# A decoder trunk's third merge: two of its four gate chunks by seven block products, ahead of the pipeline

## The chip, the cores and the metric

The kernel runs on one core of a Trainium2 chip. The metric is the device time of one execution in microseconds (us); the number given for a kernel is the median of its runs. The engines are named as in the profile: PE (TensorE, matrix products into PSUM), DVE (VectorE), ACT (ScalarE), POOL (GpSimd) and SP (SyncE, which issues most of the transfers from device memory).

## What is computed

Two layers of the same kind, on 256 tokens of width 2048 in float32. Each layer normalises its input, multiplies it by one wide input projection, and gives the parts to three token mixers: A (sparse attention), B (a convolution module) and C (stick-breaking attention). Each mixer's output is multiplied by a SiLU gate z and projected back to 2048 columns; the three results are merged by sigmoid gates, and one output projection goes into the residual:

```
y_b = (conformer_conv(ub, ...) * silu(zb)) @ w_b_out
y_c = (stick_breaking_attention(qc, kc, vc) * silu(zc)) @ w_c_out
g = sigmoid(gates).reshape(b, s, N_BRANCH, D_MODEL)
merged = g[:, :, 0] * y_a + g[:, :, 1] * y_b + g[:, :, 2] * y_c
return x + merged @ w_out
```

Here the third summand matters: per layer its gate is a product of the 256 x 2048 activations with 2048 columns of the input projection, and y_c a product of 256 x 1024 with 2048 columns.

## The kernel before

A product of float32 accuracy is made from parts. Every weight block of 256 rows x 512 columns (one **unit**, 128 partitions x 1024 elements) is loaded by SP into a `raw` buffer, rounded by ACT into `wh` (`high`, L251) and its remainder taken by DVE into `wl` (`low`, L255). The activations lie ready in the same two parts, `hx` for the normalised input. A unit's products are activations-high by `wh`, activations-low by `wh`, activations-high by `wl`, for two halves of the tokens (t = 0, 1) and two blocks of 128 rows: 12 matmuls of 128x512 (`token_products`, L265 for every matmul). There are five `raw` buffers, three pairs `wh`, `wl`, and in the pipeline (below) a fourth pair `ph`, `pl`.

The merges of branches A (b = 0) and C (b = 2) are four column chunks j of 512 columns each. Per chunk `chunk_N` makes the gate chunk `g` (8 units, K = 2048), ACT takes the sigmoid, `chunk_N` makes the y chunk (4 units, K = 1024), and DVE multiplies and adds into `mg` (`merge`, L1359 and L1360). The PSUM pool `acc` has two tiles of two banks, the pool `mm` two more. Before j = 3 of branch C stands the gate z of branch B (`gate(O_ZB, ...)`, 16 units): its product is turned over a scratch in device memory (DVE transposes, POOL transfers out and back), then comes a sigmoid on ACT and two multiplications on DVE, all some units later (`LATER`). Its factor `cv` comes from `conv_norm`, a background stage that starts at j = 2. Ahead of j = 3 stand also `hs`, the sums of blocks of `hx`.

Branch B's merge and the output projection run as one list of units (`run`), in which DVE's and SP's order is the order as written; ACT's and PE's order is set by the scheduler of the tile framework. `run` loads a unit 7 places ahead and converts it 3 places ahead. Half of each gate product there (the first 1024 rows of K, two chunks of 512 columns, two halves of tokens) is made by `seven`: seven products of sums of blocks in place of eight, with sums of activation blocks (`hs`) and of weight blocks. One block product is two half units P1a, P1b, P7a, and so on, of 6 matmuls each. Four PSUM banks X, W, Z, Y collect them, X and W in one `mm` tile, Z and Y in the other, and `combine` moves partial results between banks and the buffers V, U1, U2, R5 on DVE (L449); V is copied out by ACT after P1b (L506). Weight blocks are named by block row and column: "11" and "22" are fetched into activation slots (`fetch`, L461), "12" and "21" are loaded as units and also added to "11" by an accumulating transfer of POOL (`grow`, L490), and DVE adds or subtracts "22" (`add`, L464).

Of the kernel before, what the change touches and what calls it, by code (L numbers as in the profile page):

```python
# [14 lines left out]
P = 128  # L15
S = 256
# [32 lines left out]
def trunk(ctx: ExitStack, tc: tile.TileContext, x, w_in, xt, w_a, w_b, w_c, w_out,  # L49
# [39 lines left out]
    def nm(s):  # L89
        uid[0] += 1  # L90
        return f"{s}_{uid[0]}"

    def slot(dt=F32):
        return sp.tile([P, KC, S], dt, tag="s8", bufs=13, name=nm("s8"))

    def long_tile(name):
        return sp.tile([P, LONG], F32, tag="yT", bufs=1, name=nm(name))[:, :KC * (S + PAD)].rearrange("p (k t) -> p k t", k=KC)

    def long_slot():
        return long_tile("long")[:, :, :S]  # L100
# [97 lines left out]
    def finish():  # L198
        while stages:
            advance(stages[0])  # L200
# [129 lines left out]
    def chunk_F(w, c0, act, nk, use, later=LATER):  # L330
        turned(chunk_N(w, [(c0, 512)], act, nk), use, later)
# [40 lines left out]
    def token_products(accs, n, w_, act, k0, ku, nk, ts, banks=False):  # L372
        for i, j in ((0, 0), (1, 0), (0, 1)):
            for t, acc in zip(ts, accs):
                for k in range(ku):
                    a = part(act, i, k0 + k, 1, slice(t * P, (t + 1) * P))[:, 0, :]
                    mm = mult(acc[:, :n], a, w_[j][:, k, :], opens(acc) if banks else k0 + k == 0 and i == 0 and j == 0,
                              k0 + k == nk - 1 and j == 1)
        return mm
# [28 lines left out]

    def plain(w, c0, act, k0, accs, nk, banks=False, ts=range(NT)):
        def products(u):  # L410
            return token_products(accs(), 512, u[1:], act, k0, 2, nk, ts, banks)

        def load():
            u = load_unit(w, k0, 2, [(c0, 512)], weight_parts())
            count[0] -= 1
            return u

        return Unit(load, products)
# [17 lines left out]
    def seven(w, cols, act, sums, banks, keep, by_transfer):  # L436

        X, W, Z, Y = range(4)
        held = {}
        V, U2, U1, R5 = range(4)

        def combine(op, dst, a, b):

            dst, a, b = ({"b": banks, "k": keep}[n][0][i] for n, i in (dst, a, b))
            op(dst, a, b)  # L449

        def block(b, h):
            k, n = (int(i) - 1 for i in b)
            k = k * 4 + h * 2
            return w[k * P:(k + 2) * P, cols[n]:cols[n] + 512].rearrange("(k p) c -> p k c", p=P)

        def fetch(b):
            v = slot().rearrange("p (k a) t -> p k (a t)", a=2)
            with tc.high_priority():
                for h in range(2):
                    held[b, h] = v[:, h * 2:h * 2 + 2, :]  # L460
                    nc.sync.dma_start(held[b, h], block(b, h))  # L461

        def add(h, to, b):
            nc.vector.tensor_add(held[to, h], held[to, h], held[b, h])  # L464

        def sub(h, b, a, k0, t, bank):
            ts = slice(t * P, (t + 1) * P)

            def load():
                if (b, h) not in held:  # L470
                    k, n = (int(i) - 1 for i in b)
                    u = load_unit(w, k * 4 + h * 2, 2, [(cols[n], 512)], weight_parts())
                    count[0] -= 1
                    held[b, h] = u[0]
                    return u
                return (held[b, h], *weight_parts())

            def products(u):
                for i, j in ((0, 0), (1, 0), (0, 1)):
                    for k in range(2):  # L480
                        mm = mult(banks[0][bank], part(a, i, k0 + h * 2 + k, 1, ts)[:, 0, :], u[1 + j][:, k, :],
                                  opens(banks[0][bank]), False)
                return mm

            u = Unit(load, products)
            u.size = 0.5
            return u

        def grow(h, to, b):
            nc.gpsimd.dma_start(held[to, h], block(b, h), accum_op=ALU.add)  # L490

        p1, p2, p4 = (("11", act, 0, 0, X), ("21", act, 4, 0, X), ("11", act, 4, 1, W))
        p5, p6, p3 = (("11", sums, 4, 1, Z), ("11", sums, 0, 0, Y), ("22", sums, 4, 0, Z))
        p7 = ("12", sums, 0, 1, Y)
        order = [p1, p7, p5, p6, p3, p2, p4]
        subs = [sub(h, *v) for v in order for h in range(2)]
        P1, P7, P5, P6, P3, P2, P4 = (subs[n:n + 2] for n in range(0, 14, 2))
        for h in range(2):
            for b, last, at in (("12", P1, P7), ("22", P5, P6), ("21", P6, P4)):
                if b in by_transfer:  # L500
                    last[h].more = [partial(grow, h, "11", b)]
                else:
                    at[h].early = [partial(add, h, "11", b)]
            P7[h].early = [*P7[h].early, partial(add, h, "12", "22")]
        add_, sub_ = nc.vector.tensor_add, nc.vector.tensor_sub
        P1[1].now = [lambda: nc.scalar.copy(keep[0][V], banks[0][X])]  # L506
        P7[1].now = [partial(combine, add_, ("k", U1), ("k", V), ("b", Y))]
        P5[1].now = [partial(combine, sub_, ("k", R5), ("b", Z), ("k", V))]
        P6[1].now = [partial(combine, sub_, ("k", U1), ("b", Y), ("k", U1)),
                     partial(combine, sub_, ("k", U2), ("k", V), ("b", Y))]  # L510
        extra = {(0, 1): U2, (1, 0): U1, (1, 1): R5}
        return fetch, subs, lambda q, t: keep[0][extra[q, t]] if (q, t) in extra else None
# [115 lines left out]
    def gate(c0, o, b, w, hx, done=None, more=2):  # L628
        def use(k, y):
            sg = sigmoid_of(y)  # L630
            yield 1
            while done is not None and done.count(k // 4) < NT:
                advance(stages[0])
            nc.vector.tensor_mul(y, y, sg)
            nc.vector.tensor_mul(y, y, blocks(o[:, k:k + 4, :]).rearrange("p k u i -> p u k i"))
            split(blocks(hi(b, k, 4)), blocks(lo(b, k, 4)), by_feature(y))

        for k in range(0, KC, 4):
            chunk_F(w, c0 + k * P, hx, KD, partial(use, k), LATER + more if k else LATER - 1)

    def tap(yT, cv, pr, c, q):
        wq = pr[:, P_CW + c * TAPS + q:P_CW + c * TAPS + q + 1]
# [46 lines left out]
    for layer in range(DEPTH):  # L689
# [672 lines left out]
        for b in (0, 2):  # L1362
            gx = ga if b == 0 else gc
            for j in range(4):
                if b == 0 and j == 3:
                    gc = parts(KC)
                    gate(O_ZC, qcT, gc, w, hx, stuck)
                if b == 2 and j == 2:
                    flush()
                    start(conv_norm())  # L1370
                if b == 2 and j == 3:
                    finish()
                    gb = parts(KC)
                    gate(O_ZB, cv, gb, w, hx, more=-1)
                    hs, v = parts(KC), long_slot()
                    for i in (0, 4):
                        nc.vector.tensor_add(v[:, i:i + 4, :], hi(hx, i, 4).bitcast(F32), lo(hx, i, 4).bitcast(F32))
                    list(forms(v))
                    for i in (4, 0):
                        split_at(hs, i, 4, v[:, i:i + 4, :])  # L1380
                g = chunk_N(w, [(O_G + b * D + j * 512, 512)], hx, KD)
                sg = [ev() for _ in range(NT)]
                with tc.high_priority():
                    for t in range(NT):
                        nc.scalar.activation(sg[t], g[t], AF.Sigmoid)
                if j == 0:
                    settle()
                y = chunk_N((w_a, w_c)[b // 2][layer], [(j * 512, 512)], gx, KC)
                with tc.high_priority():
                    for t in range(NT):  # L1390
                        merge(b, j, t, y, sg)

        def banks():
            return Lazy(1, lambda: halves([mm_tile(), mm_tile()]))

        og = O_G + D
        units, woven, fetches = [], [], []
        for j in (0, 2):
# [74 lines left out]
        def accs(q):  # L1473
            if q not in acc:
                if q - p0 in (0, 1):
                    acc[q] = o_banks[0][(p0 + 1 - q) * 2:(p0 + 1 - q) * 2 + 2]
                else:
                    acc[q] = token_accs()
            return acc[q]
# [42 lines left out]
                units[n].before = [*units[n].before, partial(fetch, b)]  # L1522
        woven = sorted([*enumerate(units), *woven], key=lambda e: e[0])
        with tc.manual_schedule(engines={nc.vector.engine, nc.sync.engine}):
            run([u for _, u in woven], [])
        if not last:
            continue
        known, half = small(2), small(2)
# [109 lines left out]
```

## Time and profile before

| what | value |
|---|---|
| median of 3 runs | 2005.98 us (2005.85 to 2006.45) |
| the profiled execution's own time | 2004.83 us |
| its span in the profile | 2003.1 us |
| PE busy, matmuls | 1993.5 us (100%), 9314 |
| DVE busy, ACT busy, POOL busy | 82%, 55%, 10% |
| mean DMA rate | 232 GB/s |

The share of busy time is an average over stages. Matmuls are pipelined: one is shown with 0.39 us, but the next begins long before it ends, so the distance from start to start tells what one costs. Times of the trace are counted from the span's start. The place of the change is, in layer 0, the stretch from about 690 to 850 us, and in layer 1 the same about 1000 us later.

### The profile page before, as it was taken

The numbers are of one execution on the slowest core, as the hardware profiler recorded it, in microseconds if no ns is written. First come the engines' busy times: TensorE is split into PE (matmuls) and PEld (weight loads), VectorE is DVE, ScalarE is ACT, GpSimd is POOL, SyncE is SP. The second block draws the span as 40 slices with busy tenths as digits, with TensorE's granted clock in tenths as the row PEclk, the third lists the DMA queues.
The fourth block names the chain that finished last, engine by engine and source line by source line (L and its number), as shares of the span: only waits on it lengthen the run. The fifth ranks groups of instructions, "written<-read, shape, count | busy, mean of one in ns | idle before, by whom it ended". The sixth has DMA issues, their size and how long they took to land.

```text
span 2003.1 us, 25866 instructions
## 1 busy us (share of the span) xinstructions
PE 1993.5 (100%) x9314; PEld 1674.2 (84%) x9314; DVE 1646.5 (82%) x2179; ACT 1107.4 (55%) x1275; POOL 200.5 (10%) x308
## 2 busy tenths in 40 slices
PE   9999999999999999999999999999999999999998
PEld 8889888888888888888888988888888888888886
DVE  8667899878888877798785779988888788778997
ACT  7555555566644455565554555555656445555654
POOL 0111012100010001022110111121000100011120
PEclk9999999999999999999999999999999999999999
DMA  7788578755575567789977885787555765687894
GB/s 279 229 286 266 185 223 291 247 179 186 174 222 192 189 219 253 244 256 281 299 254 231 278 256 184 231 284 247 179 178 173 227 193 190 216 272 241 266 300 160
DMA packets 235585, 463.80 MB, mean 232 GB/s; under 512 B 17280, under 2 KB 30080, under 8 KB 235328
## 3 DMA queue, kind: packets, MB, share of 16 engines
q1 hardware_dynamic: 208768, 389.25, 59.7%
q0 software_dynamic: 25024, 69.75, 12.4%
q10 hardware_dynamic: 1664, 3.15, 0.4%
q8 instruction: 73, 1.20, 0.2%
q14 instruction: 56, 0.46, 0.1%
HBM read 429.31 MB, written 32.77 MB: 231 GB/s over the span
## 4 chain that ended last, share of the span: by engine, by line
PE 98%; DMA 1%; DVE 1%; issue 0%; POOL 0%; ACT 0%; DVEq 0%; POOLq 0%
PE acc L265 80%; PE mm L265 15%; DMA z<-zt 1%; PE mm L1078 1%; PE mm L1168 0%; DMA zy<-z 0%; PE mm L1136 0%; PE mm L1273 0%; PE mm L1219 0%; PE mm L837 0%; DVE wl L255 0%; PE mm L1249 0%; PE mm L1278 0%; PE mm L1222 0%; PE mm L1139 0%
## 5 line engine op out<-in xcount | busy, mean ns | idle before, releaser
L265 PE MATMUL acc<-wh,s 128*128 128x512 f32 (+1 forms) x4712 | 1165.8, 389 | 0.0
L251 ACT CAST wh<-raw 128x1024 fp32r<-128x1024 f32 (+1 forms) x667 | 697.9, 1048 | 704.2 <-PE acc L265 489.8
L255 DVE TENSOR_TENSOR wl<-raw,wh 128x1024 fp32r<-128x1024 f32 (+1 forms) x668 | 808.6, 1213 | 265.0 <-ACT wh L251 262.2
L265 PEld LDWEIGHTS acc<-wh,s 128*128 128x128 f32 x4712 | 876.9, 188 | 172.9 <-issue 0.2
L265 PE MATMUL acc<-wl,s 128*128 128x512 f32 (+1 forms) x2164 | 575.7, 388 | 0.3 <-DVE wl L255 0.3
L265 PEld LDWEIGHTS acc<-wl,s 128*128 128x128 f32 x2164 | 405.7, 188 | 82.6 <-DVE wl L255 0.7
L297 POOL DMA_DIRECT2D z<-zt x180 | 106.1, 602 | 1297.0 <-DVE zt L294 942.2
L647 DVE SCALAR_TENSOR_TENSOR s<-yT,cst,s 128x256 f32<-128x256 f32 x480 | 211.9, 477 | 0.0
L265 PE MATMUL mm<-wh,s 128*128 128x512 f32 x544 | 139.4, 389 | 0.0
L265 PEld LDWEIGHTS mm<-wh,s 128*128 128x128 f32 x544 | 102.1, 188 | 21.2
L265 PE MATMUL mm<-wl,s 128*128 128x512 f32 x272 | 77.7, 389 | 0.0
L265 PEld LDWEIGHTS mm<-s,wl 128*128 128x128 f32 x512 | 66.9, 191 | 5.0
L265 PE MATMUL mm<-s,wl 128*128 128x192 f32 x512 | 66.0, 271 | 0.0
L251 ACT CAST wh<-s 128x1024 fp32r<-128x1024 f32 x43 | 45.3, 1052 | 27.5 <-PE mm L265 13.3
L265 PEld LDWEIGHTS mm<-wl,s 128*128 128x128 f32 x272 | 51.1, 188 | 10.6
L303 POOL DMA_DIRECT2D zy<-z x50 | 36.1, 722 | 236.3 <-DMA z<-zt 72.7
L255 DVE TENSOR_TENSOR wl<-s,wh 128x1024 fp32r<-128x1024 f32 x43 | 52.4, 1218 | 8.9 <-ACT wh L251 8.6
L294 DVE STREAM_TRANSPOSE zt<-acc 128x512 f32<-128x512 f32 (+1 forms) x68 | 45.3, 679 | 9.4 <-PE acc L265 9.4
L251 ACT CAST ph<-raw 128x1024 fp32r<-128x1024 f32 x31 | 32.7, 1054 | 26.8 <-PE mm L265 14.6
L265 PE MATMUL mm<-ph,s 128*128 128x512 f32 x176 | 45.5, 390 | 0.0
L255 DVE TENSOR_TENSOR pl<-raw,ph 128x1024 fp32r<-128x1024 f32 x31 | 37.8, 1218 | 6.9 <-ACT ph L251 6.9
L265 PEld LDWEIGHTS mm<-ph,s 128*128 128x128 f32 x176 | 33.0, 188 | 7.2 <-issue 0.4
(293 smaller groups left out, 1378.9 us busy)
## 6 DMA issues: line engine op xcount, KB each, us to landing
raw<-in_w_in_dram SPq DMA_DIRECT2D x535, 512.0 KB, 4.3
raw<-in_w_out_dram SPq DMA_DIRECT2D x56, 512.0 KB, 6.6
zy<-z POOLq DMA_DIRECT2D x48, 512.0 KB, 5.1
z<-zt POOLq DMA_DIRECT2D x172, 128.0 KB, 4.3
raw<-in_w_a_dram SPq DMA_DIRECT2D x32, 512.0 KB, 3.6
raw<-in_w_c_dram SPq DMA_DIRECT2D x32, 512.0 KB, 4.3
raw<-in_w_b_dram SPq DMA_DIRECT2D x32, 512.0 KB, 5.7
s<-in_w_in_dram SPq DMA_DIRECT2D x16, 512.0 KB, 5.5
```

The source lines that it names most:

```text
L251: newest_parts[0] = nc.scalar.copy(u[1], u[0])
L255: newest_parts[1] = sub = nc.vector.tensor_sub(u[2], u[0], u[1].bitcast(F32))
L265: newest[0] = nc.tensor.matmul(o, lhsT, rhs, start=start, stop=stop, skip_group_check=True)
L294: nc.vector.transpose(tmp[:, t].rearrange("p b k i -> p k b i"), src.rearrange("p k (b c) -> p k b c", b=4, c=32))
L297: nc.gpsimd.dma_start(z[:, :, :, a, :].rearrange("t b c e -> c (t b) e"), tmp[a * 32:(a + 1) * 32].rearrange("c t b k i -> c (t b) (k i)"))
L303: nc.gpsimd.dma_start(y.rearrange("p (t a) k i -> p t (a k i)", a=4), z.rearrange("t b c a e -> (b c) t (a e)"))
L647: nc.vector.scalar_tensor_tensor(o, yT[:, c, q:q + S], wq, o, op0=ALU.mult, op1=ALU.add)
L1078: nc.tensor.matmul(ps[:, q * S:(q + 1) * S], qi[i][:, hd, :], ki[j][:, 0, :], start=n == 0, stop=n == 2)
```

## The change

In the loop over branch C's chunks, j = 2 becomes the last turn. It starts `conv_norm`, makes the gate z of branch B at once, then `hs`, then the two y chunks 2 and 3 (8 units, which stay in the two `acc` tiles), and leaves the loop. The two gate chunks 2 and 3 go to the front of the list of units: the first 1024 rows of K by a call of `seven` (14 half units P1a to P4b), the rest by 8 plain units, X8 to X14 for chunk 3 (banks X, W) and Z8 to Z14 for chunk 2 (banks Z, Y), in an order written by hand. Block "11" is fetched into the buffer `yT` that held the convolution's input, "22" into a slot. Sigmoids and merges follow as `gates_c` and `close_c`. The second half of gate z is used two units earlier than before.

```diff
+    def long_as_slot():
+        return sp.tile([P, LONG], F32, tag="yT", bufs=1, name=nm("block"))[:, :KC * S].rearrange("p (k t) -> p k t", k=KC)
...
         def products(u):
+            if ts == (1, 0):
+                return [token_products(accs()[t:t + 1], 512, u[1:], act, k0, 2, nk, [t], banks) for t in ts][-1]
...
-            chunk_F(w, c0 + k * P, hx, KD, partial(use, k), LATER + more if k else LATER - 1)
+            chunk_F(w, c0 + k * P, hx, KD, partial(use, k), LATER + more if k and more > 0 else LATER - 3 if k else LATER - 1)
...
                 if b == 2 and j == 2:
                     flush()
                     start(conv_norm())
-                if b == 2 and j == 3:
-                    finish()
                     gb = parts(KC)
                     gate(O_ZB, cv, gb, w, hx, more=-1)
+                    finish()
...
+                    y_c = {c: chunk_N(w_c[layer], [(c * 512, 512)], gc, KC) for c in (2, 3)}
+                    break
...
+        g_banks, kept = banks(), Lazy(1, lambda: halves([t4(), t4()]))
+        og = O_G + 2 * D
+        fetch, subs, share = seven(w, (og + 3 * 512, og + 2 * 512), hx, hs, g_banks, kept, ("12", "21"))
+        ahead = {f"P{i}{h}": subs[n * 2 + m] for n, i in enumerate((1, 7, 5, 6, 3, 2, 4)) for m, h in enumerate("ab")}
...
+        def gates_c(q, g_banks=g_banks, kept=kept, share=share):
+            for t in range(NT):
+                v, to = g_banks[0][q * 2 + t], kept[0][q * 2 + t]
+                if share(q, t) is not None:
+                    nc.vector.tensor_add(to, v, share(q, t))
+                    v = to
+                nc.scalar.activation(to, v, AF.Sigmoid)
+
+        def close_c(c, t, kept=kept):
+            merge(2, c, t, y_c[c], kept[0][(3 - c) * 2:(3 - c) * 2 + 2])
...
+        for n, v, place in (("P1a", "11", long_as_slot), ("X8", "22", slot)):
+            ahead[n].before = [partial(fetch, v, place)]
+        ahead = [ahead[n] for n in
+                 "P1a P1b X8 X10 P7a P7b X12 P5a P5b P2a P6a P6b P2b Z8 P3a Z10 P3b Z12 P4a Z14 X14 P4b".split()]
...
-            run([u for _, u in woven], [])
+            run([*ahead, *(u for _, u in woven)], [])
```

What the built programs make of it, at three places of layer 0 (layer 1 has the same order there). First ACT about the copy of V. Before, at the front of the pipeline:

```order
L251 CAST wh_6758<-s_1162_6743 128x1024 [waits DMAHW2_49,DVE_49,PE_49]
L251 CAST wh_6765<-raw_6767 128x1024 [waits DMAHW7_49,DVE_49,PE_49]
L251 CAST ph_6771<-raw_6773 128x1024 [waits DVE_49,PE_49]
L251 CAST wh_6791<-raw_6793 128x1024 [waits DVE_49,PE_49,Activation_49]
L251 CAST wh_6809<-raw_6811 128x1024 [waits DMAHW2_49,PE_49,Activation_49]
L506 COPY t_1197_6871<-mm_6834 128x512 [waits PE_49]
L251 CAST wh_6829<-s_1162_6743 128x1024 [waits DMASW6_49,PE_49,Activation_49]
```

The first row is P1b's weights, the next four are the four units that PE multiplies after P1b; the copy stands behind them. With the change, in `ahead`:

```order
L254 CAST wh_6434<-block_6429 128x1024 [waits DVE_49,PE_49]
L589 CAST s_1001_5888<-zy_6309 128x4x256 [waits DVE_49]
L511 COPY t_1129_6491<-mm_6472 128x512 [waits PE_49]
L254 CAST wh_6439<-raw_6441 128x1024 [waits DMAHW3_49,Activation_49]
L254 CAST ph_6443<-raw_6445 128x1024 [waits DMAHW4_49]
L254 CAST wh_6447<-raw_6449 128x1024 [waits DVE_49,Activation_49]
L254 CAST ph_6467<-block_6429 128x1024 [waits DMASW6_49,DVE_49,PE_49]
L254 CAST wh_6454<-raw_6456 128x1024 [waits DVE_49]
```

The rows are P1b's weights, a part of gate z, the copy of V, and the weights of X8, X10, P7a, P5a and P7b: the copy, which waits for P1b's products, now stands between P1b's weights and those of X8, the unit that PE multiplies right after P1b, and P5a's stand ahead of P7b's.

Second, PE about P6 (rows with a wait; mm_6835 before and mm_6473 now hold Z and Y, mm_6834 and mm_6472 hold X and W). Before:

```order
L265 MATMUL acc_6816<-wh_6874,s_1053_6170 128x512 [waits Activation_49]
L265 MATMUL mm_6835<-wh_6892,s_1109_6479 128x512 [waits DVE_49,Activation_49]
L265 MATMUL mm_6835<-ph_6902,s_1109_6479 128x512 [waits Activation_49]
L265 MATMUL mm_6834<-wh_6913,s_4_89 128x512 [waits Activation_49]
L265 MATMUL mm_6835<-wh_6931,s_1110_6480 128x512 [waits DVE_49,Activation_49]
```

These are a unit of branch B's y, P6a, P6b, a plain unit of X and W, and P3a. Now, and under it DVE's order at the same place:

```order
L268 MATMUL mm_6472<-wh_6538,s_3_88 128x512 [waits Activation_49]
L268 MATMUL mm_6473<-wh_6512,s_1069_6253 128x512 [waits DVE_49]
L268 MATMUL mm_6473<-ph_6528,s_1069_6253 128x512 [waits Activation_49]
L268 MATMUL mm_6472<-wl_6539,s_3_88 128x512 [waits DVE_49]
L268 MATMUL mm_6473<-wh_6551,s_4_89 128x512 [waits DVE_49]
```

```order
L469 TENSOR_TENSOR block_6429<-block_6429,s_1107_6436 128x1024 [waits DVE_49]
L258 TENSOR_TENSOR wl_6513<-block_6429,wh_6512 128x1024 [waits PE_49,Activation_49]
L258 TENSOR_TENSOR pl_6529<-block_6429,ph_6528 128x1024 [waits PE_49,Activation_49]
L454 TENSOR_TENSOR t_1130_6492<-mm_6473,t_1129_6491 128x512 [waits PE_49]
L258 TENSOR_TENSOR wl_6539<-raw_6540,wh_6538 128x1024 [waits DMAHW1_49]
L258 TENSOR_TENSOR wl_6552<-raw_6553,wh_6551 128x1024 [waits DMAHW2_49,PE_49]
L258 TENSOR_TENSOR wl_6571<-s_1107_6436,wh_6570 128x1024 [waits PE_49,Activation_49]
L454 TENSOR_TENSOR t_1130_6492<-mm_6473,t_1130_6492 128x512 [waits PE_49]
L454 TENSOR_TENSOR t_1129_6491<-t_1129_6491,mm_6473 128x512
```

PE's rows are P2b's first part, P6a, P6b, P2b's rest and Z8; DVE's are the second sum for P6, the remainders of P6a and P6b, R5, the remainders of P2b, Z8 and P3a, then U1 and U2. Whole units stood between P5b and P6a and between P6b and P3a before; now a half unit or less stands there.

Third, SP's loads. Before:

```order
L240 DMA raw_6741<-in_w_b_dram 128x2x512 [waits DMAHW3_49,DVE_49]
L461 DMA s_1162_6743<-in_w_in_dram 128x2x512 [waits DVE_49]
L240 DMA raw_6748<-in_w_b_dram 128x2x512 [waits DMAHW4_49,Activation_49]
L240 DMA raw_6754<-in_w_b_dram 128x2x512 [waits DMAHW5_49,DVE_49]
L461 DMA s_1173_6762<-in_w_in_dram 128x2x512 [waits PE_49]
```

These are a unit of branch B's y, block "11" (its first half), two more units and block "22". Now:

```order
L243 DMA raw_6404<-in_w_c_dram 128x2x512 [waits DMAHW3_49,DVE_49]
L466 DMA s_1107_6436<-in_w_in_dram 128x2x512 [waits PE_49]
L243 DMA raw_6441<-in_w_in_dram 128x2x512 [waits DMAHW4_49,DVE_49]
L243 DMA raw_6445<-in_w_in_dram 128x2x512 [waits DMAHW5_49,DVE_49]
L243 DMA raw_6449<-in_w_in_dram 128x2x512 [waits DMAHW6_49,DVE_49]
L243 DMA raw_6456<-in_w_in_dram 128x2x512 [waits DMAHW7_49,DVE_49]
L243 DMA raw_6463<-in_w_in_dram 128x2x512 [waits DMAHW0_49,DVE_49]
```

The rows are the last y unit of branch C, block "22", and the loads of X8, X10, P7a, P7b and X12, which stand behind "22". The slot of "22" is that of the first half of branch C's gated mixer output, which PE reads until the sixth of the eight y units; block "11" stands some twenty loads earlier, among those of gate z.

## Rows read from the trace of the kernel before

**Rows 1.** The page: busy time and the granted clock in 40 slices.
```profile
PE 1993.5 (100%) x9314; PEld 1674.2 (84%) x9314; DVE 1646.5 (82%) x2179; ACT 1107.4 (55%) x1275; POOL 200.5 (10%) x308
...
PEclk9999999999999999999999999999999999999999
```
**Rows 2.** Waits of PE over the whole span: us, times, longest.
```profile
PE mm L837 <- DVE eps L73: 1.1, 1, 1.1
PE acc L265 <- DVE wl L255: 0.3, 1, 0.3
```
**Rows 3.** Timeline of PE, two units: start, us, line, operation, count.
```profile
749.41 1.98 PE L265 MATMUL acc<-wh,s 128*128 128x512 f32 x8
...
752.13 1.98 PE L265 MATMUL acc<-wh,s 128*128 128x512 f32 x8
```
**Rows 4.** Timeline of PE: the starts of P5b, P6a, P6b and P3a.
```profile
816.17 1.07 PE L265 MATMUL mm<-wh,s 128*128 128x512 f32 x4
...
820.25 1.07 PE L265 MATMUL mm<-wh,s 128*128 128x512 f32 x4
...
821.61 1.07 PE L265 MATMUL mm<-ph,s 128*128 128x512 f32 x4
...
825.69 1.07 PE L265 MATMUL mm<-wh,s 128*128 128x512 f32 x4
```
**Rows 5.** Timeline of DVE about R5, U1 and U2 (in brackets idle time before).
```profile
811.72 1.22 DVE L464 TENSOR_TENSOR s<-s,s 128x1024 f32<-128x1024 f32 x1
812.86 1.22 DVE L255 TENSOR_TENSOR wl<-raw,wh 128x1024 fp32r<-128x1024 f32 x1
...
817.74 0.69 DVE L449 TENSOR_TENSOR t<-mm,t 128x512 f32<-128x512 f32 x1
...
823.59 0.68 DVE L449 TENSOR_TENSOR t<-mm,t 128x512 f32<-128x512 f32 x1
824.19 0.68 DVE L449 TENSOR_TENSOR t<-t,mm 128x512 f32<-128x512 f32 x1
```
**Rows 6.** Timeline of PE and DVE where the last y chunk of branch C ends.
```profile
790.21 1.98 PE L265 MATMUL acc<-wh,s 128*128 128x512 f32 x8
...
790.41 0.69 DVE L1359 TENSOR_TENSOR ev<-acc,ev 128x512 f32<-128x512 f32 x1 [1.31 <-PE acc L265]
791.01 1.22 DVE L255 TENSOR_TENSOR wl<-raw,wh 128x1024 fp32r<-128x1024 f32 x1
```
**Rows 7.** Timeline of ACT and DVE: a cast, its remainder, the copy of V.
```profile
786.78 1.05 ACT L251 CAST wh<-raw 128x1024 fp32r<-128x1024 f32 x1 [0.71 <-PE acc L265]
789.50 1.05 ACT L251 CAST wh<-raw 128x1024 fp32r<-128x1024 f32 x1 [1.67 <-PE acc L265]
...
803.73 1.05 ACT L251 CAST wh<-raw 128x1024 fp32r<-128x1024 f32 x1 [0.76 <-PE mm L265]
804.68 0.57 ACT L506 COPY t<-mm 128x512 f32<-128x512 f32 x1
...
787.87 1.23 DVE L255 TENSOR_TENSOR wl<-raw,wh 128x1024 fp32r<-128x1024 f32 x1 [0.54 <-ACT wh L251]
```
**Rows 8.** Timeline of SP and ACT: the fetch of "11", and its first cast.
```profile
780.63 0.88 SPq L461 DMA_DIRECT2D s<-in_w_in_dram  x2
...
784.08 1.05 ACT L251 CAST ph<-s 128x1024 fp32r<-128x1024 f32 x1 [1.44 <-DMA s<-in_w_in_dram]
```
**Rows 9.** Windows: stretch, its us, busy of five engines, clock, DMA share, GB/s.
```profile
10.00:15.00 5.00, 5.00 (x24) 4.14 (x23) 4.63 (x7) 4.81 (x10) 0.00 (x0) 1.00 1.05 407
...
790.00:805.00 15.00, 15.00 (x67) 12.26 (x66) 13.20 (x14) 7.11 (x8) 2.42 (x2) 1.00 1.04 295
```
**Rows 10.** POOL's accumulating transfers, line 490: issue to landing.
```profile
DMA to landing us min/median/max: 5.7/7.9/10.5
```
**Rows 11.** Timeline of DVE and ACT: gate z's last transpose, its sigmoid.
```profile
760.50 0.70 DVE L294 STREAM_TRANSPOSE zt<-acc 128x512 f32<-128x512 f32 x1
...
774.13 1.06 ACT L625 ACTIVATE t<-zy 128x1024 f32<-128x1024 f32 x1
```

More of the change, by code (lines that the diff above doesn't have):

```diff
@@ L454, in block, with fetch @@
             return w[k * P:(k + 2) * P, cols[n]:cols[n] + 512].rearrange("(k p) c -> p k c", p=P)
-        def fetch(b):
-            v = slot().rearrange("p (k a) t -> p k (a t)", a=2)
+        def fetch(b, place=slot):
+            v = place().rearrange("p (k a) t -> p k (a t)", a=2)
             with tc.high_priority():
@@ L1394, in banks, with g @@
             return Lazy(1, lambda: halves([mm_tile(), mm_tile()]))
+        g_banks, kept = banks(), Lazy(1, lambda: halves([t4(), t4()]))
+        og = O_G + 2 * D
+        fetch, subs, share = seven(w, (og + 3 * 512, og + 2 * 512), hx, hs, g_banks, kept, ("12", "21"))
+        ahead = {f"P{i}{h}": subs[n * 2 + m] for n, i in enumerate((1, 7, 5, 6, 3, 2, 4)) for m, h in enumerate("ab")}
+        for k in range(KC, KD, 2):
+            for q, v in enumerate("XZ"):
+                def g(q=q, g_banks=g_banks):
+                    return g_banks[0][q * 2:q * 2 + 2]
+                ahead[f"{v}{k}"] = plain(w, og + (3 - q) * 512, hx, k, g, KD, True, (1, 0) if v == "X" and k == KC else range(NT))
+        def gates_c(q, g_banks=g_banks, kept=kept, share=share):
[7 more added lines that the diff above has]
+            merge(2, c, t, y_c[c], kept[0][(3 - c) * 2:(3 - c) * 2 + 2])
+        for last_, c in (("Z14", 2), ("P4b", 3)):
+            ahead[last_].now = [*ahead[last_].now, partial(gates_c, 3 - c)]
+            ahead[last_].after = [partial(close_c, c, t) for t in reversed(range(NT))]
+        for n, v, place in (("P1a", "11", long_as_slot), ("X8", "22", slot)):
+            ahead[n].before = [partial(fetch, v, place)]
+        ahead = [ahead[n] for n in
+                 "P1a P1b X8 X10 P7a P7b X12 P5a P5b P2a P6a P6b P2b Z8 P3a Z10 P3b Z12 P4a Z14 X14 P4b".split()]
         og = O_G + D
```

## The prediction, made before the changed kernel ran

> **What bounds the kernel now.** I read the page first: PE is busy for all of the span and its granted clock is the full one in every slice [rows 1]. A busy PE need not be a PE at its peak, so the waits of PE come next: 1.4 us in the whole span, all but 0.3 of it at the start [rows 2]. Then PE's timeline: a unit of 12 matmuls starts 2.72 us after the one ahead of it [rows 3], so one matmul of 128x512 costs 0.227 us, in the chunks as in the pipeline, where P5b, a whole unit and P6a follow each other at 1.36 + 2.72 us [rows 4]. PE does nothing but multiply, without gaps. A change can therefore win only by fewer matmuls, and any wait that it puts in front of PE is lost in full.
>
> **The change, part by part.** I count time from the start of P1a in one layer; both layers have the same order there, so each sum counts twice.
>
> *Matmuls.* The first halves of two gate chunks cost 8 units x 12 = 96 matmuls before and 14 half units x 6 = 84 now. 12 x 0.227 = 2.72 us per layer are saved, 5.44 us in all. `ahead` needs 14 x 1.36 + 8 x 2.72 = 40.8 us of PE, where the same chunks took 43.5.
>
> *Gate z, moved.* Its 16 units cost PE the same in the new place, and SP and POOL issue the same transfers for them; `conv_norm` has 16 units beside it instead of 12. I cost this at nothing: what hides it is the path of its second half, which took 774.13 - 761.20 = 12.9 us from the last transpose to the sigmoid [rows 11], and now has the eight y units, 21.8 us. If it came late, P1a's remainder would wait behind z's multiplications on DVE. `hs` only comes earlier. Block "11" is asked for some twenty loads ahead, so P1a and P1b are ready.
>
> *X8.* ACT's order has the copy of V between the weights of P1b and those of X8. The copy must wait for P1b's last product; such an engine starts 0.20 us after PE could start its next matmul [rows 6]. P1b's slot ends at 2.72, so the copy runs from 2.92; it takes 0.57 us, a neighbour on ACT starts 0.1 before the last one's end, and X8's cast takes 1.05 [rows 7]: ready at 4.45, while PE stands since 2.72. DVE begins the remainder 0.04 after the cast's end and takes 1.23 [rows 7], until 5.7; X8's first four matmuls are through at 5.4. Stalls of 1.8 and 0.3, together 2.1 us. Before, the copy stood behind four units' casts and cost PE nothing.
> This rests on ACT not letting the cast pass the copy. The rows show it for DVE only: a remainder whose cast ended at 790.55 [rows 7] started at 791.01, after a merge that had waited for PE [rows 6]. The Trainium skill, page "TensorE: Matmul & The Clock Gate", section "Architectural detail", says that ACT and DVE take their instructions strictly in order. If ACT could swap the two, this stall would go and the sum below would be 4.2 us lower, 2011.4; I take the order as it stands.
>
> *P5 and P6.* From 4.5 on, DVE is the slower engine. Its order up to R5 has 14 operations of 1024 elements at 1.14 us from start to start and two of 512 at 0.6 [rows 5]: 17.2 us. Two waits for ACT come on top. P5a's cast stands ahead of P7b's and must wait until X10 has freed the buffer `ph`, which makes P7b's remainder 1.4 late; and P6b's cast stands behind those of P2b and Z8, which costs 0.8. R5 so ends at about 24.0. P6a's first product waits for DVE, although its own weights come from ACT: it writes the tile of Z and Y, which R5 reads. Without waits PE would reach P6a at 4.5 + 0.3 + 3 x 2.72 (X8, X10, X12) + 4 x 1.36 (P7, P5) + 1.36 (P2a) + 0.9 (part of P2b) = 20.7. So 3.3 us are lost here, some 0.4 of it already at P5a and P2b. If both waits for ACT were hidden, 1.0 us would be left: 4.5 + 17.2 against 20.7. Before, a whole unit stood in between: R5 started at 817.74, and P6a only at 820.25 [rows 4, 5].
>
> *Z8.* It too writes a tile that DVE must first read, for U1 and U2, and after P6b PE has only the last two matmuls of P2b, 0.45 us. The two subtractions take 0.6 + 0.68 and start 0.2 after P6b's end at the earliest [rows 5, 6]: at least 1.05 us of stall. But P3a's remainder stands ahead of them and needs a buffer that P6a frees. P6a runs from 24.0 to 25.4, its buffer is free at 25.6; with the cast the remainder ends at 27.4, the subtractions at 28.6, and PE stands from 27.2: 1.5 us. Before, a unit of X and W stood here: the subtractions ended at 824.87 for P3a at 825.69 [rows 4, 5].
>
> *The end of `ahead`.* Branch B's first y unit needs the `acc` tile of y chunk 2, free when DVE has done, after Z14: two additions, a merge, a remainder and one multiplication, about 0.2 + 0.6 + 0.6 + 1.3 + 1.1 + 0.7 = 4.5 us. X14 and P4b cover 4.08: 0.5 us. At best nothing.
>
> *Loads.* 8 loads go and 12 transfers come per layer: 8 for the four blocks, 4 accumulating ones on POOL. "22" waits on SP for a slot that PE frees 5.4 us ahead of P1a, and the loads of X8 to X12 wait behind it; before, SP waited for a slot too, but PE's next units were already loaded. A first transfer landed 3.4 us after its issue [rows 8]; later ones follow by 512 KB at 295 to 407 GB/s [rows 9], 1.3 to 1.8 us each. X8's weights, the third, land by 1.8, ahead of the cast; P7a's, the fifth, by 3.3 to 5.4, just ahead of DVE's use at 5.6, but two accumulating transfers share the rate. P5a's sum has 13 us, and such transfers took 10.5 at most [rows 10]. I take nothing; at worst P7a's weights come 2 us late, and the chain to R5 by as much.
>
> *The rest.* In the pipeline every fourth unit is now another one's place for `ph`; the smallest slack seen there is 0.8 us [rows 4, 5]. I take nothing.
>
> **The sum.** Stalls of 2.1 + 3.3 + 1.5 + 0.5 = 7.4 us against 2.72 saved: 4.7 us per layer, 9.4 in all. The profiled execution took 2004.83 (span 2003.1), so 2014.2; the median of the runs is 1.15 higher, which gives **2015.4 us**.
>
> **Rivals.**
> 1. *Only the fixed waits count*: DVE's backlog is hidden. Stalls of 2.1 + 1.0 + 1.05 = 4.2, less 2.72: +1.4 per layer, 2.9 in all, **2008.9**. For it: I counted every hand-over at its full length. Against: ACT's order puts P5a's and P6b's casts where they hold up others.
> 2. *Faster.* One place decides: if DVE's and ACT's work for P1b to P2b ran so early that the copy was the only thing left, and X8 could start as soon as P1b ends, the saved matmuls would show, less the 1.05 at Z8: 2 x (2.72 - 1.05) = 3.3, **2002.6**; with Z8 covered as well 5.4, 2000.5. For it: PE bounds the kernel, and no such unit has ever made it wait [rows 2, 3]. It needs X8's cast ahead of the copy, that is, less than 2.7 us of stalls per layer; the order says otherwise.
> 3. *Late weights.* "22" holds SP, the burst of seven loads shares the rate with the accumulating transfers, and P7a, P7b and X12 come 1.5 us late each before DVE can go on: 3 us more per layer (the rest falls into waits already counted), **2021.4**. For it: at 295 GB/s the DMA engines are full [rows 9]. Against: ACT and DVE are late anyway.
> 4. *The clock falls.* The granted clock is full in every window of the trace [rows 1, 9], where PE never paused. The Trainium skill, page "TensorE: Matmul & The Clock Gate", section "HAM oscillation", says that gaps between bursts of matmuls can put PE back to its half clock; no run here shows it after a pause. A unit at half clock would take another 2.72 us; after two of the pauses per layer that makes 10.9 more, **2026**.
>
> **Chances.** Forecast 0.65, rival 1 0.14, rival 2 0.05, rival 3 0.13, rival 4 0.03. A measurement of this kernel can tell 0.2%, 4.0 us, from no change: 2002.0 to 2010.0. Rival 1 lies inside, rival 2 at its edge; so faster 0.03, same 0.15, slower 0.82. The forecast's own terms run from 2010 (one of the waits for ACT hidden, the end covered) to 2019.4 (P7a's weights 2 us late). The range takes in rivals 1 and 3: 2008 to 2021.5.
>
> **What would show it.** PE's waits, empty now, should name ACT's cast `wh` at X8 (about 1.8 us) and DVE's subtraction into `t` at P6a and Z8 (2.9 and 1.5), in both layers, and `ahead` should take 48 us instead of 40.8. In ACT's timeline the copy should start just after P1b's last matmul, with idle time ahead of it. 9290 matmuls show the saving. No wait at X8, or a total of PE's waits under 5.4 us, would prove me wrong; a wait for a DMA at P7a or X12 would speak for rival 3, a lower clock for rival 4.

## The result, and the profile after

| | median of the runs | profiled execution | its span |
|---|---|---|---|
| before | 2005.99 us (2005.85 to 2006.45) | 2004.83 | 2003.1 |
| changed | 2022.0 us (2021.13 to 2022.67, 4 runs) | 2022.21 | 2020.4 |

The ratio is 1.0079 (95% interval 1.0062 to 1.0097): slower by 16.0 us. The forecast was 2015.4, slower by 9.4, with a range up to 2021.5. The sign and the places are right; the size is not, and the time lies 0.5 us above the range.

The page's line of PE, where [rows 1] had 9314 matmuls:

```profile
PE 1995.1 (99%) x9290; PEld 1670.9 (83%) x9290; DVE 1678.2 (83%) x2213; ACT 1119.9 (55%) x1289; POOL 210.4 (10%) x316
```

The 24 matmuls are gone. PE's waits over the span (us in total, times, longest), which held 1.4 us in [rows 2]:

```profile
PE mm L268 <- DVE t L454: 7.3, 4, 2.5
PE mm L268 <- ACT wh L254: 3.6, 3, 1.6
PE mm L268 <- DVE pl L258: 2.8, 2, 1.6
PE acc L268 <- DVE t L1364: 1.1, 2, 0.6
```

The first two rows and the last are the forecast ones (P6a and Z8; X8, with one wait of 0.36 us in the pipeline; the end). The third, for a remainder `pl`, was not forecast. It is at X10, as PE's timeline in layer 0 shows (in brackets the idle time before, and its releaser):

```profile
746.58 1.07 PE L268 MATMUL mm<-wh,s 128*128 128x512 f32 x4
...
751.08 1.20 PE L268 MATMUL mm<-wh,s 128*128 128x512 f32 x4 [1.62 <-ACT wh L254]
752.34 0.89 PE L268 MATMUL mm<-wl,s 128*128 128x512 f32 x2
753.03 1.91 PE L268 MATMUL mm<-wh,s 128*128 128x512 f32 x4
754.74 1.05 PE L268 MATMUL mm<-wl,s 128*128 128x512 f32 x2
755.59 2.27 PE L268 MATMUL mm<-ph,s 128*128 128x512 f32 x8
759.43 1.20 PE L268 MATMUL mm<-pl,s 128*128 128x512 f32 x4 [1.57 <-DVE pl L258]
...
774.07 1.19 PE L268 MATMUL mm<-wh,s 128*128 128x512 f32 x4 [2.54 <-DVE t L454]
...
778.86 2.12 PE L268 MATMUL mm<-wh,s 128*128 128x512 f32 x8 [1.32 <-DVE t L454]
...
798.76 2.11 PE L268 MATMUL acc<-wh,s 128*128 128x512 f32 x8 [0.56 <-DVE t L1364]
```

These are P1a, X8 (four rows), X10 (two), P6a, Z8 and branch B's first unit. Two things are new. Four matmuls of X8 took 754.74 - 753.03 = 1.71 us where four take 0.91 at the 0.227 us each of [rows 3]. And X10 waited for its own remainder. ACT's cast for it and DVE's timeline say why (the last row but one is layer 1's counterpart of DVE's second):

```profile
753.28 1.04 ACT L254 CAST ph<-raw 128x1024 fp32r<-128x1024 f32 x1 [2.25 <-DMA raw<-in_w_in_dram]
...
751.06 1.22 DVE L258 TENSOR_TENSOR wl<-raw,wh 128x1024 fp32r<-128x1024 f32 x1 [4.46 <-ACT wh L254]
757.01 1.23 DVE L469 TENSOR_TENSOR raw<-raw,s 128x1024 f32<-128x1024 f32 x1 [4.73 <-DMA raw<-in_w_in_dram]
758.16 1.22 DVE L258 TENSOR_TENSOR pl<-raw,ph 128x1024 fp32r<-128x1024 f32 x1
...
773.33 0.68 DVE L454 TENSOR_TENSOR t<-mm,t 128x512 f32<-128x512 f32 x1
...
1759.89 1.23 DVE L469 TENSOR_TENSOR raw<-raw,s 128x1024 f32<-128x1024 f32 x1 [2.83 <-DMA raw<-in_w_in_dram]
...
1776.20 0.68 DVE L454 TENSOR_TENSOR t<-mm,t 128x512 f32<-128x512 f32 x1
```

DVE's second row is P7a's sum of "12" and "22". It stands ahead of X10's remainder (third row), whose cast had ended at 754.3, and it waited for its weights until 757.01, 10.4 us after P1a's start; in layer 1 it is 1759.89 - 1751.35 = 8.5 (why less, no view shows). The forecast had 5.6. From there DVE has one more gap (0.8 us, for P6b's cast, as forecast) up to R5, which ends 27.4 and 25.5 us after P1a instead of 24.0. Of the sum's delay of 4.8 and 2.9 us, 1.4 took the place of the forecast wait for P5a's cast, which no longer shows.

The slow matmuls are the clock. The windows of the two stretches (us, busy of five engines, granted clock, DMA share, GB/s):

```profile
752.80:756.20 3.40, 3.40 (x10) 2.63 (x9) 0.00 (x0) 1.04 (x1) 0.00 (x0) 0.51 1.10 263
1776.70:1780.10 3.40, 3.16 (x8) 2.48 (x9) 2.45 (x3) 1.05 (x2) 1.08 (x1) 0.51 1.02 151
```

The granted clock was 0.51, that is 1.2 of 2.4 GHz, once per layer: in layer 0 right after the pause at X8, in layer 1 after that at P6a. The row PEclk of [rows 1] could not show this: its slices are 50 us long, and the changed kernel's page has a 9 in each of them too. In windows of 1.7 us, the kernel before has the full clock up to its last matmul, which ends at 1994.9 us, and the half one at its end, from 1999 us on.

Per layer, from P1a to branch B's first unit, against the 40.8 us of matmuls:

| us | forecast | layer 0 | layer 1 |
|---|---|---|---|
| X8 | 2.1 | 1.62 | 1.62 |
| X10 and P7a | 0 | 1.72 | 1.27 |
| P5a to P6a | 3.3 | 2.54 | 2.55 |
| Z8 | 1.5 | 1.32 | 0.93 |
| end | 0.5 | 0.56 | 0.56 |
| what no row shows as a wait | 0 | 3.6 | 3.6 |
| sum | 7.4 | 11.4 | 10.6 |

The last row but one is what is left of 798.76 - 746.58 = 52.2 and 1802.71 - 1751.35 = 51.4: the half clock, X8's stall ahead of its products with `wl` (752.34 - 751.08 - 0.91 = 0.35), and a little at each pause. Less the 2.72 saved, the two layers give 16.5 us.

### The profile page after: what moved, and what is told of

Same layout as the page of the kernel before. It is cut to its first block, busy times and chain, and to the rows that moved or that the text cites. A ratio compares the mean times of both kernels' runs of the same rounds, so it can differ in the third digit from the quotient of the medians.

```text
span 2020.4 us, 25896 instructions
## 1 busy us (share of the span) xinstructions
PE 1995.1 (99%) x9290; PEld 1670.9 (83%) x9290; DVE 1678.2 (83%) x2213; ACT 1119.9 (55%) x1289; POOL 210.4 (10%) x316
## 4 chain that ended last, share of the span: by engine, by line
PE 94%; DMA 2%; DVE 1%; issue 1%; ACT 1%; POOL 0%; SPq 0%; DVEq 0%; POOLq 0%; ACTq 0%
PE acc L268 74%; PE mm L268 17%; DMA raw<-in_w_in_dram 1%; DMA zy<-z 1%; PE mm L1083 1%; PE mm L1173 0%; DVE wl L258 0%; ACT wh L254 0%; PE mm L1224 0%; PE mm L1278 0%; PE mm L1141 0%; DVE pl L258 0%; DMA z<-zt 0%; PE mm L842 0%; PE mm L1254 0%
## 5 line engine op out<-in xcount | busy, mean ns | idle before, releaser
L268 PE MATMUL acc<-wh,s 128*128 128x512 f32 (+1 forms) x4464 | 1104.5, 389 | 1.1 <-DVE t L1364 1.1
L254 ACT CAST wh<-raw 128x1024 fp32r<-128x1024 f32 (+1 forms) x651 | 680.2, 1047 | 672.8 <-PE acc L268 433.2
L258 DVE TENSOR_TENSOR wl<-raw,wh 128x1024 fp32r<-128x1024 f32 (+1 forms) x652 | 789.6, 1214 | 236.3 <-ACT wh L254 233.1
L268 PEld LDWEIGHTS acc<-wh,s 128*128 128x128 f32 x4464 | 830.3, 188 | 164.9 <-DVE t L1364 2.0
L268 PE MATMUL acc<-wl,s 128*128 128x512 f32 (+1 forms) x2040 | 542.6, 388 | 1.1 <-DVE wl L258 1.1
L268 PEld LDWEIGHTS acc<-wl,s 128*128 128x128 f32 x2040 | 382.5, 188 | 78.4 <-DVE wl L258 1.5
L268 PE MATMUL mm<-wh,s 128*128 128x512 f32 x704 | 183.8, 393 | 10.9 <-DVE t L454 7.3
L268 PEld LDWEIGHTS mm<-wh,s 128*128 128x128 f32 x704 | 132.5, 189 | 41.4 <-DVE t L454 9.0
L268 PE MATMUL mm<-wl,s 128*128 128x512 f32 x352 | 102.6, 394 | 0.4 <-DVE wl L258 0.2
L268 PE MATMUL mm<-ph,s 128*128 128x512 f32 x256 | 65.9, 391 | 0.0
L268 PEld LDWEIGHTS mm<-ph,s 128*128 128x128 f32 x256 | 48.7, 190 | 10.4
```

Source lines behind the costliest of these rows:

```text
L254: newest_parts[0] = nc.scalar.copy(u[1], u[0])
L258: newest_parts[1] = sub = nc.vector.tensor_sub(u[2], u[0], u[1].bitcast(F32))
L268: newest[0] = nc.tensor.matmul(o, lhsT, rhs, start=start, stop=stop, skip_group_check=True)
```

## The experiments

Theory 1: the fifth load behind "22" is late, and DVE's order passes that on to X10 and R5. Rivals: the waits count each for itself, as the forecast added them; the moved gate costs something; the half clock is the loss. Each group of runs has its own time of before on the same chip: 2005.15 us for the first four kernels, 2005.48 for the next three, 2005.28 for the last. Gains are differences to it; the change stands 16.0 above.

**The chunks without the seven products.** The 22 entries of `ahead` become 16 plain units, and the blocks' fetches and the sums of partial results go:

```diff
-                 "P1a P1b X8 X10 P7a P7b X12 P5a P5b P2a P6a P6b P2b Z8 P3a Z10 P3b Z12 P4a Z14 X14 P4b".split()]
+                 "Z0 Z2 Z4 Z6 Z8 Z10 Z12 Z14 X0 X2 X4 X6 X8 X10 X12 X14".split()]
```

> The changed kernel with the two gate chunks at the same place ahead of the pipeline, but by 16 plain units each of two token halves (Z0 to Z14, then X0 to X14), without the seven block products; gate z stays moved. It has the matmuls of the kernel before. Theory: moving gate z and the chunks is free, all of the loss is in the seven products: 2006 us (2005 to 2007.5). Rival: the moved gate or the list of units itself has a price, over 2008.

Measured: 2005.32 us, ratio 1.0000 (0.9991 to 1.0010). Moving gate z and the chunks is free; all of the loss belongs to the seven products, with their transfers and their order.

**"22" two loads later.**

```diff
-        for n, v, place in (("P1a", "11", long_as_slot), ("X8", "22", slot)):
+        for n, v, place in (("P1a", "11", long_as_slot), ("P7a", "22", slot)):
```

> One edit to the changed kernel: block '22' is fetched two loads later, behind the loads of X8 and X10 instead of ahead of them. SP so no longer holds these two back behind the slot that '22' waits for, P7a's weights are the third of the burst behind the slot and no longer the fifth, and ACT's order now has X8's cast ahead of the copy of V. Theory 1 (late weights: in the changed kernel P7a's weights were first used 10.4 us after the start of P1a, and X10's remainder stands behind that sum on DVE): seven transfers took 15.7 us there, two fewer ahead are 4.5 us, so P7a's sum no longer holds X10; the wait at X8 (1.6) goes too. What is left are the DVE backlog at P6a (about 3.7 per layer as PE comes there earlier), 1.5 at Z8, 0.5 at the end: 5.7 less 2.72 saved, 3.0 per layer, 2012 us (2009 to 2015). Rival (the copy alone counts, the weights would have been hidden): X8's 1.6 per layer go and nothing else, 2018.8.

Measured: 2015.03 us, 1.0047 (1.0030 to 1.0064): 9.9 above before, 3 more than expected. PE's timeline at X8, P6a and Z8 (P1a starts at 747.55), and a window behind P6a:

```profile
751.11 1.19 PE L268 MATMUL mm<-wh,s 128*128 128x512 f32 x4 [0.68 <-ACT t L511]
...
770.46 1.19 PE L268 MATMUL mm<-wh,s 128*128 128x512 f32 x4 [2.55 <-DVE t L454]
...
776.20 2.14 PE L268 MATMUL mm<-wh,s 128*128 128x512 f32 x8 [0.67 <-DVE t L454]
...
771.00:776.00 5.00, 4.53 (x13) 3.11 (x11) 4.03 (x5) 3.04 (x3) 0.29 (x1) 0.66 1.08 208
```

The wait at X10 is gone, P6a starts 22.9 us after P1a instead of 27.5, and X8 waits 0.68 for the copy of V itself. About 2 of the missing 3 us are the clock: after P6a's pause it fell to half in both layers, and from P6a to Z8 PE worked 776.20 - 770.46 - 0.67 = 5.1 us where the kernel with P5a's cast behind P7b's (below), with the clock full, worked 3.5. Some of that comes back at once, because Z8 then waits less for DVE: from P6a to Z8 it is 5.7 and 6.0 us in the two layers, there 4.9.

**The copy of V alone.** It is issued behind X8's cast; SP's order stays:

```diff
+        def copy_v(kept=kept, g_banks=g_banks):
+            with tc.issue_after(casts[id(x8[0][1])].ins):
+                nc.scalar.copy(kept[0][0], g_banks[0][0])
...
+        ahead["P1b"].now = [copy_v]
```

> One edit to the changed kernel: ACT's copy of V is put behind X8's cast; SP's order, with '22' ahead of X8, stays. Theory 1 (late weights decide): PE's wait at X8 (1.6 us) goes, but X10's remainder still waits behind the sum for P7a, whose weights come when they came, so PE waits that much longer there: 2022 us (2020.5 to 2022.7). Rival (each wait counts by itself, as my prediction's sum had it): 1.6 less per layer, 2018.8.

Measured: 2022.99 us, 1.0089 (1.0074 to 1.0104). PE's timeline at X8 and X10:

```profile
750.26 1.20 PE L269 MATMUL mm<-wh,s 128*128 128x512 f32 x4 [0.70 <-ACT t L1436]
...
759.10 1.56 PE L269 MATMUL mm<-pl,s 128*128 128x512 f32 x4 [3.31 <-DVE pl L259]
```

0.9 us less at X8 came back as 1.7 more at X10. With the weights late, the wait at X8 is worth nothing, and adding it to the others, as the forecast did, was wrong in the changed kernel. What "22" two loads later gains comes with the loads.

**Without the accumulating transfers of "12"** (P5 then multiplies "11" alone, so chunk 3's gate is another one).

```diff
+        for n in ("P1a", "P1b"):
+            ahead[n].more = []
```

> One edit to the changed kernel: the two accumulating transfers per layer that add block '12' to '11' are left out (P5 is then multiplied by '11' alone, so chunk 3's gate is another one). Theory 1, as contention: '22' and the five loads behind it then have the rate to themselves; the transfers of the queue took 1.3 us each where no accumulating transfer ran (744.3 to 745.6) and 2.5 to 4 where two did, so P7a's weights come about 7 us earlier, X10 no longer waits, and R5 comes at my forecast's 24 us instead of 26.7: 4 us less per layer, 2014 us (2011 to 2016). Rival (the block on SP alone makes the weights late): less than 1 us per layer, 2020 to 2022. PE should also show no fall of its clock if the wait at X10 goes.

Measured: 2019.67 us, 1.0075 (1.0060 to 1.0090): 14.5 above before, where 8 were expected. The weights did come early. The view of `raw` for the loads of X8 to X12, first with the change, then in this kernel:

```profile
DMA to landing us min/median/max: 6.5/12.9/14.4
```

```profile
DMA to landing us min/median/max: 6.5/7.2/8.8
```

Load by load, from issue and time to landing, X8's weights landed 2.2 us after P1a in the change, about as forecast (1.8); X10's and P7a's came 4.4 and 3.7 us after the one ahead, while the two accumulating transfers were under way, and the next two 1.3 us apart. So the accumulating transfers are what made the burst slow; "22" holding SP only made it a burst. But the time hardly followed, and the expectation of a full clock failed, as windows of this kernel show:

```profile
753.00:756.40 3.40, 3.40 (x9) 2.63 (x8) 3.40 (x4) 1.04 (x1) 0.00 (x0) 0.51 0.69 180
773.50:776.90 3.40, 3.40 (x9) 2.64 (x8) 2.44 (x3) 2.50 (x3) 0.00 (x0) 0.50 1.10 206
```

The clock fell twice per layer, after X8 and after P6a, and now PE worked all through both stretches. With X10 slow, P5a's cast waited for its buffer, and P6a started 25.8 us after P1a, 1.8 behind the forecast; from P6a to Z8 it took 6.0 us where 4.9 is the time with a full clock (below). Without these 1.8 and 1.1, `ahead`, here 798.39 - 746.71 = 51.7 us, would have taken 48.8, an estimate. The forecast had 48.2 for weights in time and a full clock. The profile is of the slowest of the four runs (2022.95 us, mean granted clock 0.995; the others 0.996 and 0.997), so the median run lost less to the clock.

**P5a's cast behind P7b's**, on top of "22" two loads later:

```diff
-        with tc.high_priority():
+        with tc.high_priority(), tc.issue_after(newest_parts[0].ins) if id(u[1]) in in_turn else nullcontext():
             newest_parts[0] = nc.scalar.copy(u[1], u[0])
...
+            in_turn.add(id(u[1]))
...
+        ahead["P5a"].load = load_p5
```

> The kernel of e1_22_later with one more edit: on ACT the cast for P5a, which waits until X10 has freed its buffer, is put behind the casts of P7b and X12 instead of ahead of P7b's. In e1_22_later DVE idled 2.34 us there and PE waited 2.55 us for R5 at P6a, after which the granted clock was half for 3.4 us, 1.7 us lost per layer. Theory (DVE's chain up to R5, held up by that cast, sets P6a): R5 comes 2.3 us sooner, the wait at P6a shrinks to 0.3; 2 x 2.25 less is 2010.5 us, and 2007.2 if the clock then stays full. Rival (DVE is just as full without that wait, since the remainders behind it pile up on the subtraction for U1): less than 0.5 us per layer, 2014 us.

Measured: 2010.4 us, 1.0025 (1.0015 to 1.0035). PE's timeline at P6a and Z8, and the window over the list:

```profile
768.30 1.20 PE L269 MATMUL mm<-wh,s 128*128 128x512 f32 x4 [1.51 <-DVE t L455]
...
773.19 2.08 PE L269 MATMUL mm<-wh,s 128*128 128x512 f32 x8 [1.41 <-DVE t L455]
...
745.00:795.00 50.00, 45.85 (x199) 36.69 (x198) 40.80 (x41) 26.86 (x28) 4.11 (x4) 1.00 0.90 269
```

That this is the 2010.5 expected is luck: the clock stayed full in both layers (mean granted clock 0.999 against 0.997), and for that case 2007.2 was expected. P6a starts 768.30 - 747.08 = 21.2 us after P1a, 1.7 sooner and not 2.25, and of the 1.6 us that the full clock gives behind P6a, 0.7 goes into Z8's wait: 0.67 behind a slow PE, it is 1.41 behind a fast one, the forecast's 1.5.

**Another order**, on top of "22" two loads later: "P5b X14 P6a P6b P2a P2b Z8 P3a Z10 P3b Z12 Z14 P4a P4b".

> The kernel of e1_22_later with another order of the units: X14 stands between P5b and P6a, where P2a stood, P2a and P2b stand together between P6b and Z8, and the end is Z12, Z14, P4a, P4b. Theory (the waits at P6a and Z8 are DVE's work of some length against what PE has in between): at P6a PE comes 1.36 us later, so 2.55 becomes 1.2; at Z8 PE has 2.7 us in place of 0.5, so 0.7 to 0.9 becomes 0; at the end PE has 2.7 instead of 4.1 ahead of branch B's first unit, so 0.56 becomes 1.9. Sum 0.8 us less per layer, 2013.4 us; if the shorter wait at P6a lets the clock stay full, 1.7 less per layer again, 2010. Rival (the wait at P6a is one for the weights of P6 or for the clock and not for R5 against PE's place): 2015 or more.

Measured: 2023.48 us, 1.0092 (1.0076 to 1.0107); a miss. PE's timeline at P6a, at P4b (two rows) and at branch B's first unit, and a window there:

```profile
769.40 1.20 PE L268 MATMUL mm<-wh,s 128*128 128x512 f32 x4 [1.05 <-DVE t L454]
...
792.03 1.20 PE L268 MATMUL mm<-wh,s 128*128 128x512 f32 x4 [1.14 <-ACT wh L254]
795.08 1.22 PE L268 MATMUL mm<-wl,s 128*128 128x512 f32 x2 [1.85 <-DVE wl L258]
798.27 3.55 PE L268 MATMUL acc<-wh,s 128*128 128x512 f32 x8 [1.97 <-DVE t L1364]
...
794.60:801.40 6.80, 4.35 (x9) 2.98 (x10) 4.23 (x6) 1.04 (x1) 1.19 (x1) 0.50 0.87 199
```

P6a waits 1.05 (1.2 expected) and Z8 no longer, so these two are what the theory says. The end costs 5.0 us and not 1.9: sigmoids, sums and merges of both chunks now fall together on ACT and DVE, ahead of P4b's own weights. The half clock began after the first of these pauses and lasted 6.8 us in each layer.

**Cover for every hand-over**, on top of "22" two loads later: the last two units of y chunk 3 (C4 and C6, which write `acc`) stand in the list.

```diff
-                    y_c = {c: chunk_N(w_c[layer], [(c * 512, 512)], gc, KC) for c in (2, 3)}
+                    y_c = {c: token_accs() for c in (2, 3)}
+                    for c, k in ((2, 0), (3, 0), (2, 4)):
+                        chunk_N(w_c[layer], [(c * 512, 512)], gc, KC, accs=y_c[c], ks=(k, k + 4))
...
+        for k in (4, 6):
+            ahead[f"C{k}"] = plain(w_c[layer], 3 * 512, gc, k, lambda y=y_c[3]: y, KC)
...
+                 "P1a P1b C4 X8 X10 P7a P7b X12 P5a P5b X14 P6a P6b P2a P2b Z8 P3a Z10 P3b Z12 Z14 P4a C6 P4b".split()]
```

> The kernel of e1_22_later with cover for every hand-over: the last two units of branch C's last y chunk (they write acc, not the banks) become units of the list, one between P1b and X8, one between P4a and P4b at the end; X14 stands between P5b and P6a, P2a and P2b between P6b and Z8. The matmuls stay those of the changed kernel. Theory (all of the loss is waits at four hand-overs, and PE's clock falls only after waits): X8 0, Z8 0, end 0, P6a 0 to 2: 2006 less 5.4 saved and at most 4 lost, 2000.5 to 2005 us, 2002.5 as a point; granted clock 1.00 all through if no wait exceeds 1 us. Rival (late weights again, or DVE too full in the whole stretch): new waits in the pipeline behind, 2008 or more.

Measured: 2006.01 us over 11 runs (2003.05 to 2007.7), 1.0001 (0.9992 to 1.0010). Its profiled execution, 2003.05, lies in the expected 2000.5 to 2005, with PE waits of 0.2 to 0.6 us left and the clock full; the median does not. Eight of the other ten runs took 2 to 5 us more, and what they lost no profile shows.

**And gate z's second half later**, taken up behind P6:

```diff
-LATER + more if k and more > 0 else LATER - 3 if k else LATER - 1
+LATER + more if k and more > 0 else LATER + 6 if k else LATER - 1
```

> The kernel of e6_cover with the second half of gate z taken up nine units later, behind P6 and not in the middle of the list. In e6_cover its three DVE operations (748.2 to 753.3, 1.4 us of idle time among them) stood ahead of X12's remainder, DVE reached the sums for P6 late, and PE still waited 0.2 and 0.6 us for DVE and ACT. Theory (DVE's work up to R5 is what is left of the price): no wait over 0.3 us in the list in either layer, 1 to 2 us below e6_cover: 2004 us against 2005.5 of the kernel before on the same chip, 0.9985 to 0.9995. Rival (e6_cover's own waits are too small to matter, and what keeps its runs 3 us above its profiled one is something else): the same ratio as e6_cover, 1.000.

Measured: 2002.32 us over 11 runs against 2005.28, ratio 0.9986 (0.9977 to 0.9995): faster than the kernel before by 3.0 us, and 19.0 below the change. PE's waits over the span:

```profile
PE mm L842 <- DVE eps L73: 1.1, 1, 1.1
PE acc L268 <- DVE t L1364: 0.7, 2, 0.3
PE mm L268 <- ACT wh L254: 0.6, 1, 0.6
PE acc L268 <- DVE wh L844: 0.2, 1, 0.2
PE acc L268 <- ACT wh L254: 0.2, 1, 0.2
```

Inside the lists of both layers only the end's 0.33 is left, and the list takes 46.7 us where the kernel above, with the same matmuls, took 48.5. That fits the theory that DVE's work in the dense stretch was the rest of the price; the gain, 3.5 us from median to median, is more than the 1 to 2 expected.

## Why the prediction was right in its sign and wrong in its size

1. *Matmuls*: right. 24 fewer; the last kernel keeps 3.0 of the 5.4 us.
2. *Gate z moved, at nothing*: right, shown by the chunks without the seven products.
3. *X8*: mechanism and size right: ACT's cast stood behind the copy, and 1.62 and 0.35 us of stalls make 2.0 for 2.1. But it could not be added to the rest: cut to 0.7 alone it gave nothing.
4. *Loads, "I take nothing"*: **the step that failed.** P7a's weights were expected 3.3 to 5.4 us after P1a, at worst 2 us later, and were used at 10.4 and 8.5. I divided the bytes by 295 to 407 GB/s and took the two accumulating transfers as sharers of that rate. Without them the five loads land in 6.5 to 8.8 us, with them in up to 14.4. [rows 10] gave how long such transfers take themselves, not what they do to the loads beside them. DVE's order, which I had counted operation by operation, put P7a's sum ahead of X10's remainder, so the delay reached PE at X10, and R5 came 3.4 and 1.5 us late. That is rival 3's mechanism, priced there at 2021.4 and held at 0.13, because "ACT and DVE are late anyway": they were late behind the weights, not beside them. Only one of their waits for ACT, 1.4 us, was hidden by the weights.
5. *P5 and P6*: right in mechanism and, with weights in time and less the clock, near in size (48.8 us of `ahead`, the estimate above, against 48.2). The wait for ACT that I named, P5a's cast ahead of P7b's, was shown by moving it.
6. *Z8 and the end*: 1.3 and 0.9 for 1.5, and 0.56 for 0.5; 1.41 with a full clock.
7. *The clock*, rival 4, held at 0.03 on the word of [rows 1], whose slices are too long to show a fall: it did fall, in all the kernels here but those whose pauses in `ahead` were the shortest (the cast behind P7b's, the two with cover, the plain units). My price of 2.72 us for a fall was too high: one that PE works through takes 1.6 to 1.7 us of its time, and behind P6a a shorter wait at Z8 gives some of that back. The Trainium skill, page "TensorE: Matmul & The Clock Gate", section "HAM oscillation", says that gaps between bursts of matmuls bring the half clock; the traces agree in kind, here with waits of 1.1 to 3.3 us for other engines, though not every such wait brought it. In layer 0 of the change the fall lay ahead of X10's wait, so a faster PE would only have waited longer; in layer 1 it followed P6a, and from there to Z8 took 5.9 us, 1.1 more than in layer 0.
8. *Restarts*, not forecast: where the clock stayed full, `ahead` took 793.04 - 747.08 = 46.0 us, 5.2 above 40.8, with four waits of 4.15 us in the rows. Each pause costs some 0.25 us more than its wait shows: 0.16 because a row counts the wait from the shown end of a matmul, 0.39 us after its start, where the next could begin after 0.227, and about 0.1 in the first matmuls behind the pause.

In the profiled execution the lists lost 16.5 us and not 9.4, so 7.1 are to be explained (6.6 in the medians). P6a started 27.5 and 25.6 us after P1a and not 24.0: 3.5 and 1.6, the late weights. From P6a to the end it was 24.7 and 25.8 and not 24.2: 0.5 in each layer for the pauses, and 1.1 for the clock's fall in layer 1 (7.1 in all before rounding). That the weights were late, and through the accumulating transfers, is shown; the split is worked out from these rows and was not tried part by part. Late weights and clock cannot be taken out one by one: without the accumulating transfers the median gained 1.5 us only, since the fall behind X8 then held up the same stretch.

## What to carry to other kernels

Where a load waits for a buffer on an in-order queue, count all loads that are let go with it, and price them by a row in which the same kinds of transfers ran side by side; then follow the DVE or ACT order from the first late operand, since work that is ready stands behind it. A hand-over of a PSUM bank needs a whole unit that writes another accumulator behind it; units of another chunk were the cover that worked here. Where PE has no gaps, waits do not add: removing one that lies ahead of a later limit gives nothing, and a pause can cost clock on top.

## What was not expected of the hardware

Two accumulating transfers of 512 KB slowed a burst of loads by more than their own bytes: in the stretch of the change in which they ran, the DMA engines were full (share 1.10) at 263 GB/s, where the same burst without them ran at 340 to 426 (744 to 752 us), and the median load took 12.9 us to land instead of 7.2. The clock fell after pauses of 1.62 us in one layer and not after the same pause in the other (layer 1 of the change, X8), so a pause's price is not the same from place to place.
